# Exponent of the cumulative decays behind the key norms' logarithm, and the last products of the second rotated query part done token tile by token tile

## The chip, the cores and the metric

The kernel runs on one core of one Trainium2 chip. The metric is the device time of one execution in microseconds (us); the time before is the median of three runs. Five engines work side by side and meet through semaphores: TensorE (PE; its weight loads are PEld), VectorE (DVE), ScalarE (ACT), GpSimd (POOL) and SyncE (SP). Each engine executes its own instructions in the order in which they stand.

## The reference, cut to what matters

Two layers of an encoder on 256 tokens and 1024 channels, all in float32. A layer normalises x, multiplies it by one large matrix `w_in` and splits the result into the inputs of two branches and their gates:

```python
h = rmsnorm(x, norm_w[l])
proj = h @ w_in[l]
(q_a, k_a, v_a, ab_a, z_a, q_b, k_b, v_b, z_b, gate_a, gate_b) = jnp.split(proj, SPLIT_IDX, axis=-1)
y_a = gated_delta_branch(q_a, k_a, v_a, ab_a, z_a, ...)       # conv of width 5 + silu, l2norm, delta rule
y_b = diff_attention_branch(q_b, k_b, v_b, z_b, cos, sin, ...) # partial rotation, two softmaxes
merged = sigmoid(gate_a) * (y_a @ w_pa[l]) + sigmoid(gate_b) * (y_b @ w_pb[l])
x = x + merged @ w_out[l]
```

In the first branch, g is the running sum of the log decays inside a chunk. Its exponent scales queries and keys (`q_c * jnp.exp(g_c)`, `kb * jnp.exp(g)`), the exponents of its differences weigh the products of keys with keys and of queries with keys, and q and k are divided by their norms. In the second branch the first 16 of each 64 columns of q_b and k_b are rotated by the token's position.

## The kernel before, in words

**Products.** A float32 product is made from three products of rounded parts: high by high, high by low, low by high. `weights()` (L273) fetches 256 rows of 512 columns of the matrix as one piece `raw` through SP's queue (L304); a copy makes the high part `hi` (L308, on ScalarE, or on VectorE for the pieces listed in `turned`), and VectorE subtracts it for the low part `lo` (L310). Four such pieces, kp 0 to 3, make one projection of 512 columns; each holds two of the eight row tiles kt. There are two buffers for `hi`, two for `lo`, three for `raw`.

`proj_tm` (L315) makes a projection with tokens on the partitions. It has one accumulator in PSUM for each of the two token tiles m = 0, 1 and runs, for each kt, three products for m = 0 and three for m = 1 (L324 to L326). `proj_fm` (L374) makes a projection with features on the partitions for the convolution; its products are L385, L387 and L389. The accumulators come from a PSUM pool of four banks (`ps_p`, L81), which the big projections take in turn, two at a time. A projection can start only when the last reader of the bank that it gets is done.

**Convolution** (`conv`). Each 256-column block of an accumulator `pf_q`, `pf_k` or `pf_v` is read by one ScalarE instruction (L675, `cvq` for the queries) and by four of VectorE (L679, the other four taps, each on top of the one before; their widths are 254, 255, 255 and 254, in an order that the scheduler picks). Then come the tanh on ScalarE (L685, `thq`) and one VectorE instruction (L690, into `kq`).

**Rotated parts** (`qk_part(s_, i)`, L594; s_ = 0 queries, 1 keys; i the half of the columns). A projection `pp_qk` by `proj_tm`; ScalarE copies each accumulator to `stg` (L597), VectorE rotates it (L602 to L605), TensorE transposes it into `qkt` (L608), ScalarE copies the result to `qkT` (L610).

**Decays.** `gates()` (L754) makes the running sums of the log decays with a minus sign, `ngc`, and at its end their exponents: `E_` on ScalarE (L777; the trace calls the tile E) and `nE` = -E_ on VectorE (L778). Both are tiles of 128 x 32. `log_decays()` (L735) takes the keys' sums of squares (`ssk`), forms `kss` in a buffer that the trace calls `ge`, takes its logarithm on ScalarE (L742), and combines it with the gates and `ngc` into `lnc` (L744, L746). `decays()` (L809) takes 32 exponents of 128 x 128 tiles of `B` with `lnc` as bias (L818), held back by `cut` until the first transposes of `qk_part(0, 0)` are out; `weigh_k()` (L821) adds two of them (`dsum`) and multiplies the products of keys with keys into `A`. `E_` and `nE` are read only by the chunks of the delta rule, far later.

ScalarE has to load a table when it changes between the logarithm and the group of exponent and tanh; the compiled program holds these loads as instructions of their own, under the line of the function that needs them.

**Order.** The tile framework schedules: it takes the program below, priorities (`tc.high_priority`) and its own costs, and writes one fixed order for each engine; `behind(x)` adds a dependency on the instruction x. PSUM banks are given out in that order too. For each layer the program reads: convolution of the keys, `gates()`, a value projection, `lambdas()`, `spread()`, `log_decays()`, convolution of the queries (first half, `pf_q`), `qk_part(0, 0)`, the decays with `weigh_k`, the second half of the query convolution, `qk_part(0, 1)`, the convolution of the values (`pf_v`), `qk_part(1, 0)` and so on; after these come the z projections (`pp_zb`, `pp_za`) with the attention's scores (`sc`, L1060), their maxima (`mx`, L1068) and exponents (`es`).

Of the kernel before, what the change touches and what calls it, by code (L numbers as in the profile page):

```python
# [11 lines left out]
AF = mybir.ActivationFunctionType  # L12
ALU = mybir.AluOpType
# [4 lines left out]
P = 128  # L18
DM = 1024
KT = DM // P  # L20
# [8 lines left out]
HP = None  # L29
# [20 lines left out]
def hybrid_encoder(  # L50
# [19 lines left out]
    V, S, G, T = nc.vector, nc.scalar, nc.gpsimd, nc.tensor  # L70
# [15 lines left out]
    def bank(name):  # L86
        return ps_m.tile([P, 512], F32, tag="m", name=name)
# [10 lines left out]
    def mid(ap, n):  # L98
        return ap.unsqueeze(1).to_broadcast([ap.shape[0], n] + list(ap.shape[1:]))
# [4 lines left out]
    mark = {}  # L104
# [165 lines left out]
    def behind(ins):  # L270
        return nullcontext() if ins is None else tc.issue_after(ins)
# [41 lines left out]
                yield 2 * kp + k, hi[:, k, :n], lo[:, k, :n]  # L313

    def proj_tm(act, w, c0, n, evac, nm, places=(None,) * 4, spare=(), later=None, turned=(), between=None,  # L315
                banks=None, held=None, first=(), raws={}):

        accs = (banks or banks2)(f"pp_{nm}")
        for kt, hi, lo in weights(w, c0, n, nm, places, later=later, spare=spare, turned=turned, held=held,
                                  first=first, raws=raws):  # L320
            for m in range(NM):
                ts_ = slice(m * P, (m + 1) * P)
                o = accs[m][:, :n]
                T.matmul(o, act[kt // 4][:, 0, kt % 4, ts_], hi, start=kt == 0, stop=False)  # L324
                T.matmul(o, act[kt // 4][:, 0, kt % 4, ts_], lo, start=False, stop=False)  # L325
                mark["proj"] = T.matmul(o, act[kt // 4][:, 1, kt % 4, ts_], hi, start=False,  # L326
                                        stop=kt == KT - 1).ins
                mark["done", nm, kt] = mark["proj"]
        if between:
            between()  # L330
        for m in range(NM):
            evac(m, accs[m][:, :n])
# [174 lines left out]
    for l in range(DEPTH):  # L507
# [86 lines left out]
        def qk_part(s_, i):  # L594
                def evac_qk(m, ps):
                    st = work.tile([P, 512], F32, tag="w2a", name=f"stg{l}{s_}{i}{m}", bufs=2)
                    S.copy(st, ps)  # L597
                    g_ = st.rearrange("p (g e) -> p g e", e=DH)
                    x12 = g_[:, :, 0 : 2 * RD].rearrange("p g (x r) -> p g x r", x=2)
                    both = lambda t_: mid(mid(t_[:, m, :], 2), 8)  # L600
                    r4 = small.tile([P, 2, 8, 2, RD], F32, tag="r4", name=f"r4{l}{s_}{i}{m}", bufs=1)
                    V.tensor_tensor(r4[:, 0], x12, both(cos), ALU.mult)  # L602
                    V.tensor_tensor(r4[:, 1], x12, both(sin), ALU.mult)
                    V.tensor_tensor(x12[:, :, 0], r4[:, 0, :, 0], r4[:, 1, :, 1], ALU.subtract)
                    V.tensor_tensor(x12[:, :, 1], r4[:, 0, :, 1], r4[:, 1, :, 0], ALU.add)  # L605
                    pt = bank(f"qkt{l}{m}{s_}{i}")
                    for b in range(4):
                        T.transpose(pt[:, b * P : (b + 1) * P], st[:, b * P : (b + 1) * P], ident)  # L608

                    mark["qkT", m] = S.mul(qkT[i][:, s_, :, m * P : (m + 1) * P],  # L610
                                           pt.rearrange("p (b t) -> p b t", b=4), (DH ** -0.5, 1.0)[s_]).ins
                proj_tm(hT, wl, (C_QB, C_KB)[s_] + 512 * i, 512, evac_qk, f"qk{l}{s_}{i}",
                        turned=(0, 1) if (s_, i) == (0, 1) else ())

# [13 lines left out]
        for kt in range(KT):  # L628
            for part in range(2):
                T.matmul(abp[0:64, :SEQ], wabr[:, kt, :], hT[kt // 4][:, part, kt % 4, :],  # L630
                         start=kt == 0 and part == 0, stop=kt == KT - 1 and part == 1)
# [3 lines left out]
        for m in range(NM):  # L635
            T.matmul(abq[:, m * 32 : (m + 1) * 32], abT[:, m * P : (m + 1) * P], id2,
                     start=True, stop=True)
# [93 lines left out]
        nE = small.tile([P, 4, NH], F32, tag="nE", name=f"nE{l}")  # L731
        ngc = small.tile([P, 4, NH], F32, tag="ngc", name=f"ngc{l}")
        E_ = small.tile([P, 4, NH], F32, tag="E_", name=f"E_{l}")

        def log_decays():  # L735
            kss = e_[:, :, 32:40]
            V.tensor_scalar(kss, ssk, 4.0 * EPS, None, ALU.add)
            kh = small.tile([P, NM, NH], F32, tag="kh", name=f"kh{l}")
            V.tensor_scalar(kh, kss, 1.0 / 16.0, None, ALU.mult)
            G.tensor_tensor(nrm.rearrange("p m h -> p (m h)"), kh.rearrange("p m h -> p (m h)"),  # L740
                            phalf, ALU.pow)
            S.activation(kss, kss, AF.Ln)  # L742
            for d in range(2):
                V.scalar_tensor_tensor(lnc[:, d], ev[:, :, d * 8 : d * 8 + 8], -1.0, kss,  # L744
                                       ALU.mult, ALU.subtract)
            V.tensor_tensor(lnc.rearrange("p d c h -> p (d c) h"), lnc.rearrange("p d c h -> p (d c) h"),  # L746
                            ngc, ALU.add)
# [6 lines left out]
        def gates():  # L754
            with behind(mark[f"k{l}1", 0][0]):
                S.activation(ev, ev, AF.Ln)
            V.scalar_tensor_tensor(ev, a_, 0.0, ev, ALU.max, ALU.add)
            glog = small.tile([P, NM, 16], F32, tag="glog", name=f"glog{l}")
            V.tensor_tensor(glog, ev[:, :, 16:32], mid(nega, NM), ALU.mult)

            gr_ps = bank(f"grps{l}")
            for d in range(2):
                for c in range(NM):
                    dc = 2 * d + c
                    T.matmul(gr_ps[0:8, dc * P : (dc + 1) * P], glog[:, c, d * 8 : d * 8 + 8],
                             tri[:, d, :], start=True, stop=True)
            grow = work.tile([8, 4, P], F32, tag="w2c", name=f"grow{l}", bufs=3)
            with behind(mark[f"k{l}1", 3][1]):
                V.tensor_copy(grow.rearrange("h c i -> h (c i)"), gr_ps[0:8, :])
            gv = gdr.rearrange("c h d i -> h d c i")  # L770
            for d in range(2):
                G.dma_start(out=gv[:, d], in_=grow[:, 2 * d : 2 * d + 2])
            gc_ps = bank(f"gcps{l}")
            for dc in range(4):
                T.transpose(gc_ps[:, dc * 8 : dc * 8 + 8], grow[:, dc, :], ident[:8, :8])
            V.tensor_scalar(ngc, gc_ps[:, :32].rearrange("p (c h) -> p c h", c=4), -1.0, None, ALU.mult)
            S.activation(E_, ngc, AF.Exp, scale=-1.0)  # L777
            V.tensor_scalar(nE, E_, -1.0, None, ALU.mult)  # L778


        A = big.tile([P, 2, NM, 4, P], F32, tag="A", name=f"A{l}")
# [327 lines left out]
        def z_part(z, c_base, nm, i):  # L1109
            def evac_z(m, ps):  # L1110
                silu2(z[i][:, m, :], ps)
            proj_tm(hT, wl, c_base + 512 * i, 512, evac_z, f"{nm}{l}{i}",
                    banks=None if i or nm == "za" else banks2_c)
# [6 lines left out]
        with tc.high_priority(offset=HP):  # L1120
            gates()
        for _ in proj_by_tile(hT, wl, C_VB + 512, evac_v(1), f"vb{l}1", places2, spare=range(4),
# [4 lines left out]
                              held={} if l else dict.fromkeys(range(2), mark[f"k{l}0", 1][0])):  # L1127
            pass
        lambdas()
        spread()  # L1130
        log_decays()
        conv("q", C_QA, 1, 0)
        qk_part(0, 0)
        cut = mark["qkT", 0]
        decays(0, 0)
# [8 lines left out]
        conv("q", C_QA, 1, 1)  # L1144
        take_blocks()
        qk_part(0, 1)
        conv("v", C_VA, None, 0)
        qk_part(1, 0)
        substitute(f"qk{l}10")
        conv("v", C_VA, None, 1)  # L1150
# [141 lines left out]
        def evac_o(i):  # L1292
            def evac(m, ps, cs=slice(0, 512)):
# [7 lines left out]
                held={2: mark["load", f"pb{l}1", 1], 3: mark["load", f"pb{l}1", 3]})  # L1301
# [81 lines left out]
```

## Time and profile before

| what | value |
|---|---|
| median of three runs (751.34, 753.07, 753.03) | 753.03 us |
| the profiled execution | 751.43 us |
| its span, first to last instruction | 749.7 us |
| granted TensorE clock, mean | 0.997 |
| busy: PE, DVE, ACT, POOL | 739.6, 586.4, 480.9, 139.0 us |

The span is 1.7 us shorter than the execution's own time. Times in rows are microseconds from the span's start; a row shows start, duration, engine, line, operation, output and inputs, and in brackets for how long the engine stood idle before it and what released it. Instructions of one engine overlap a little in the rows, so that the distance from start to start is what an instruction takes from its engine's time, and it is shorter than the duration. PE is busy almost throughout, so what counts is where PE waits, and for whom.

### The profile page before, as it was taken

To read this page: it belongs to the slowest core of one execution; us is meant where nothing else is said; L and a number is where in the kernel's file an instruction comes from. 1 tells how busy PE (TensorE), PEld (TensorE's weight loads), DVE (VectorE), ACT (ScalarE), POOL (GpSimd) and SP (SyncE) were. 2 spreads that over 40 slices of the span, in tenths; PEclk is the share of its full clock that TensorE was granted. 3 is DMA by queue.
4 is the path that set the end of the run, shared out by engine and by line. 5 is a ranking of instruction groups with operands and counts; after the bars stand their busy time and mean duration, and the time that the engine had idled before them with its cause. 6 is when DMAs were issued, how large, how long until landed. Compare 5 with 4: busy or idle time off the path is not lost.

```text
span 749.7 us, 13916 instructions
## 1 busy us (share of the span) xinstructions
PE 739.6 (99%) x5176; PEld 641.2 (86%) x5176; DVE 586.4 (78%) x1109; ACT 480.9 (64%) x1022; POOL 139.0 (19%) x221
## 2 busy tenths in 40 slices
PE   8999999999999999999999999999999999999996
PEld 6999899987888889888889889889778888998885
DVE  8696898999985965578667769999999669537782
ACT  6657775667876576645456578555787757566552
POOL 5004111112022440100000150202110425301000
PEclk9999999999999999999999999999999999999998
DMA  8755566776666462567674466767666747336641
GB/s 260 238 169 169 167 171 199 212 209 198 208 182 177 151 181 84 170 199 245 202 232 134 130 189 174 216 178 233 199 171 194 197 129 234 94 114 200 218 143 57
DMA packets 73734, 135.46 MB, mean 181 GB/s; under 512 B 12944, under 2 KB 13921, under 8 KB 73666
## 3 DMA queue, kind: packets, MB, share of 16 engines
q1 hardware_dynamic: 64750, 113.65, 50.3%
q0 software_dynamic: 7936, 19.35, 8.8%
q10 hardware_dynamic: 980, 1.58, 0.6%
q8 instruction: 41, 0.67, 0.4%
q14 instruction: 27, 0.22, 0.1%
HBM read 125.53 MB, written 9.01 MB: 179 GB/s over the span
## 4 chain that ended last, share of the span: by engine, by line
PE 95%; DVE 1%; issue 1%; ACT 1%; DMA 1%; SPq 0%; POOLq 0%; POOL 0%; DVEq 0%; ACTq 0%
PE pp_vb L369 4%; PE pp_qk L325 4%; PE pp_qk L326 3%; PE pp_qk L324 3%; PE sc L1060 2%; PE pp_o L369 2%; PE pf_k L385 2%; PE pp_za L325 2%; PE pf_v L385 2%; PE pf_v L389 2%; PE pp_gb L324 2%; PE pp_gb L325 2%; PE pp_zb L324 2%; PE pf_q L387 2%; PE pf_k L387 2%; PE pf_v L387 2%
## 5 line engine op out<-in xcount | busy, mean ns | idle before, releaser
L325 PE MATMUL pp_qk<-lo_qk,hT 128*128 128x512 f32 x128 | 50.5, 395 | 1.1 <-DVE lo_qk L310 1.1
L326 PE MATMUL pp_qk<-hi_qk,hT 128*128 128x512 f32 x128 | 49.9, 390 | 0.0
L310 DVE TENSOR_TENSOR lo_qk<-raw_qk,hi_qk 128x1024 fp32r<-128x1024 f32 x32 | 39.0, 1220 | 11.8 <-ACT hi_qk L308 11.6
L324 PE MATMUL pp_qk<-hi_qk,hT 128*128 128x512 f32 x128 | 45.4, 395 | 0.0
L308 ACT CAST hi_qk<-raw_qk 128x1024 fp32r<-128x1024 f32 x28 | 29.4, 1049 | 22.9 <-PE pp_qk L326 7.1
L1070 ACT ACTIVATE es<-sc,mx 128x256 f32<-128x256 f32 x64 | 29.6, 474 | 19.6 <-DVE mx L1068 19.6
L310 DVE TENSOR_TENSOR lo_pb<-raw_pb,hi_pb 128x1024 fp32r<-128x1024 f32 x16 | 19.6, 1224 | 21.2 <-ACT hi_pb L308 20.9
L387 PE MATMUL pf_q<-hT,hi_q 128*128 128x256 f32 x128 | 36.1, 286 | 0.0
L385 PE MATMUL pf_k<-hT,hi_k 128*128 128x256 f32 x128 | 36.0, 287 | 0.0
L385 PE MATMUL pf_v<-hT,hi_v 128*128 128x256 f32 x128 | 35.8, 285 | 0.0
L387 PE MATMUL pf_v<-hT,hi_v 128*128 128x256 f32 x128 | 35.8, 284 | 0.0
L385 PE MATMUL pf_q<-hT,hi_q 128*128 128x256 f32 x128 | 35.8, 284 | 0.0
L387 PE MATMUL pf_k<-hT,hi_k 128*128 128x256 f32 x128 | 35.7, 283 | 0.0
L389 PE MATMUL pf_q<-hT,lo_q 128*128 128x256 f32 x128 | 35.1, 287 | 0.0
L389 PE MATMUL pf_v<-hT,lo_v 128*128 128x256 f32 x128 | 34.5, 287 | 0.0
L389 PE MATMUL pf_k<-hT,lo_k 128*128 128x256 f32 x128 | 34.3, 283 | 0.0
L308 ACT CAST hi_pa<-raw_pa 128x1024 fp32r<-128x1024 f32 x16 | 16.9, 1055 | 22.2 <-PE pp_pa L326 16.0
L679 DVE SCALAR_TENSOR_TENSOR cvq<-pf_q,cw,cvq 128x254 f32<-128x254 f32 (+1 forms) x64 | 29.9, 477 | 0.9 <-ACT cvq L675 0.2
L325 PEld LDWEIGHTS pp_qk<-lo_qk,hT 128*128 128x128 f32 x128 | 24.0, 188 | 7.4 <-DVE lo_qk L310 2.4
L679 DVE SCALAR_TENSOR_TENSOR cvv<-pf_v,cw,cvv 128x254 f32<-128x254 f32 (+1 forms) x64 | 29.7, 474 | 0.1
L679 DVE SCALAR_TENSOR_TENSOR cvk<-pf_k,cw,cvk 128x254 f32<-128x254 f32 (+1 forms) x64 | 29.0, 477 | 1.0 <-ACT cvk L675 0.2
L310 DVE TENSOR_TENSOR lo_pa<-raw_pa,hi_pa 128x1024 fp32r<-128x1024 f32 x16 | 19.6, 1224 | 11.2 <-ACT hi_pa L308 11.2
(414 smaller groups left out, 2536.9 us busy)
## 6 DMA issues: line engine op xcount, KB each, us to landing
raw_qk<-in_w_in_dram SPq DMA_DIRECT2D x32, 512.0 KB, 3.8
raw_k<-in_w_in_dram SPq DMA_DIRECT2D x16, 512.0 KB, 4.5
raw_q<-in_w_in_dram SPq DMA_DIRECT2D x16, 512.0 KB, 3.7
raw_v<-in_w_in_dram SPq DMA_DIRECT2D x16, 512.0 KB, 3.8
raw_zb<-in_w_in_dram SPq DMA_DIRECT2D x16, 512.0 KB, 3.7
raw_za<-in_w_in_dram SPq DMA_DIRECT2D x16, 512.0 KB, 3.7
raw_ga<-in_w_in_dram SPq DMA_DIRECT2D x16, 512.0 KB, 4.7
raw_pb<-in_w_pb_dram SPq DMA_DIRECT2D x16, 512.0 KB, 3.9
```

The source lines that it names most:

```text
L308: high = (V.tensor_copy if kp in turned else S.copy)(hi[:, :, :n], raw[:, :, :n]).ins
L310: mark[nm, kp] = high, V.tensor_tensor(lo[:, :, :n], raw[:, :, :n], hi[:, :, :n].bitcast(F32), ALU.subtract).ins
L324: T.matmul(o, act[kt // 4][:, 0, kt % 4, ts_], hi, start=kt == 0, stop=False)
L325: T.matmul(o, act[kt // 4][:, 0, kt % 4, ts_], lo, start=False, stop=False)
L326: mark["proj"] = T.matmul(o, act[kt // 4][:, 1, kt % 4, ts_], hi, start=False, stop=kt == KT - 1).ins
L369: mark["proj"] = T.matmul(o, act[kt // 4][:, pa, kt % 4, ts_], ws[kt][1 + pw], start=kt == 0 and n_ == 0, stop=kt == KT - 1 and n_ == 2).ins
L385: T.matmul(o, hi[:, cs], act[kt // 4][:, 0, kt % 4, :], start=first, stop=False, skip_group_check=True)
L387: T.matmul(o, hi[:, cs], act[kt // 4][:, 1, kt % 4, :], start=False, stop=False, skip_group_check=True)
L389: T.matmul(o, lo[:, cs], act[kt // 4][:, 0, kt % 4, :], start=False, stop=done, skip_group_check=True)
L679: V.scalar_tensor_tensor(ca[:, o0:o1], acc[:, b, o0 + sft : o1 + sft], cw[:, j, cb : cb + 1], ca[:, o0:o1], ALU.mult, ALU.add)
L1060: mm = T.matmul(sp[n][:, qt * SEQ : (qt + 1) * SEQ], qkT[h // 4][rows, 0, h % 4, qt * P : (qt + 1) * P], qkT[h // 4][rows, 1, h % 4, :], s ...
L1070: S.activation(es[:, n, qt, :], spv[:, qt, :], AF.Exp, bias=mx[:, n, qt : qt + 1], accum_out=s_all[:, h, n, qt : qt + 1])
```

## The change

Two edits. First, `E_` and `nE` leave the end of `gates()`. They now stand in `log_decays()`, right behind the logarithm of `kss`; `E_` with a dependency on that logarithm and with high priority, `nE` with neither. Second, `proj_tm` gets an argument `ends`, which only `qk_part(0, 1)` sets: the products of the last two row tiles (kt 6 and 7) are written as six for token tile 0 and then six for token tile 1, instead of three and three alternating.

```diff
     def proj_tm(..., banks=None, held=None, first=(), raws={}, ends=False):
+        ending = []
         accs = (banks or banks2)(f"pp_{nm}")
         for kt, hi, lo in weights(...):
+            last_ = [(kt, hi, lo)]
+            if ends and kt >= KT - 2:
+                ending.append((kt, hi, lo))
+                if kt < KT - 1:
+                    continue
+                last_ = ending
             for m in range(NM):
-                ts_ = slice(m * P, (m + 1) * P)
-                o = accs[m][:, :n]
-                T.matmul(...)   # three products
+                for kt, hi, lo in last_:
+                    ts_ = slice(m * P, (m + 1) * P)
+                    o = accs[m][:, :n]
+                    T.matmul(...)   # three products
...
                 proj_tm(hT, wl, (C_QB, C_KB)[s_] + 512 * i, 512, evac_qk, f"qk{l}{s_}{i}",
-                        turned=(0, 1) if (s_, i) == (0, 1) else ())
+                        turned=(0, 1) if (s_, i) == (0, 1) else (), ends=(s_, i) == (0, 1))
...
-            S.activation(kss, kss, AF.Ln)
+            with behind(S.activation(kss, kss, AF.Ln).ins), tc.high_priority(offset=HP):
+                S.activation(E_, ngc, AF.Exp, scale=-1.0)
+            V.tensor_scalar(nE, E_, -1.0, None, ALU.mult)
...
             V.tensor_scalar(ngc, gc_ps[:, :32]..., -1.0, None, ALU.mult)
-            S.activation(E_, ngc, AF.Exp, scale=-1.0)
-            V.tensor_scalar(nE, E_, -1.0, None, ALU.mult)
```

Lines behind the first edit move down by 8, so L685 becomes L693 and so on. Each engine has as many instructions as before; POOL's order is unchanged, and on SP only two loads of `raw_za` change places. On the other three engines the scheduler moves rows in many places. The following are the ones that the prediction speaks of, from layer 0.

**Place A, ScalarE, about 77 us in the trace of before: logarithm, table load, tanh of the first query block.** `ge` is the buffer of `kss`, and the number behind a name is that of a buffer. Before:

```order
L742 ACT_TABLE_LOAD
L742 ACTIVATE ge_347<-ge_347 128x2x8 [waits DVE_49]
L685 ACT_TABLE_LOAD [waits DVE_49]
L685 ACTIVATE thq_996<-cvq_990 128x256 [waits Activation_49]
L675 ACTIVATE cvq_999<-pf_q_868,cw_300 128x256
L308 CAST hi_qk_1062<-raw_qk_1064 128x1024 [waits DMAHW7_49,PE_49]
```

Now:

```order
L750 ACT_TABLE_LOAD
L750 ACTIVATE ge_347<-ge_347 128x2x8 [waits DVE_49]
L751 ACT_TABLE_LOAD
L751 ACTIVATE E_369<-ngc_368 128x32
L693 ACTIVATE thq_996<-cvq_990 128x256 [waits DVE_49,Activation_49]
L683 ACTIVATE cvq_999<-pf_q_868,cw_300 128x256
L308 CAST hi_qk_1062<-raw_qk_1064 128x1024 [waits DMAHW7_49,PE_49]
```

The second table load no longer waits for VectorE; the wait is on the tanh alone, and `E_` stands between.

**Place A, VectorE, beside it.** Before:

```order
L679 SCALAR_TENSOR_TENSOR cvq_990<-pf_q_868,cw_300,cvq_990 128x255 [waits DVE_49]
L744 SCALAR_TENSOR_TENSOR lnc_366<-ge_347 128x16 [waits Activation_49]
L744 SCALAR_TENSOR_TENSOR lnc_366<-ge_347 128x16
L679 SCALAR_TENSOR_TENSOR cvq_990<-pf_q_868,cw_300,cvq_990 128x254 [waits DVE_49]
L746 TENSOR_TENSOR lnc_366<-lnc_366,ngc_368 128x32 [waits DVE_49]
```

Now:

```order
L687 SCALAR_TENSOR_TENSOR cvq_990<-pf_q_868,cw_300,cvq_990 128x255 [waits DVE_49]
L754 SCALAR_TENSOR_TENSOR lnc_366<-ge_347 128x16 [waits Activation_49]
L754 SCALAR_TENSOR_TENSOR lnc_366<-ge_347 128x16
L752 TENSOR_SCALAR nE_367<-E_369 128x32 [waits Activation_49]
L687 SCALAR_TENSOR_TENSOR cvq_990<-pf_q_868,cw_300,cvq_990 128x254 [waits DVE_49]
L756 TENSOR_TENSOR lnc_366<-lnc_366,ngc_368 128x32 [waits DVE_49]
```

`nE`, which waits for `E_`, now stands ahead of the last tap of `cvq_990`, on which the tanh depends.

**Place C, VectorE, about 105 to 110 us: the low parts of the last two pieces of `qk_part(0, 1)` and the first block of the second query half (`cvq_1323`).** Before:

```order
L310 TENSOR_TENSOR lo_qk_1397<-raw_qk_1398,hi_qk_1396 128x1024 [waits DMAHW7_49,Activation_49]
L679 SCALAR_TENSOR_TENSOR cvq_1323<-pf_q_1201,cw_300,cvq_1323 128x255 [waits DVE_49] x2
L679 SCALAR_TENSOR_TENSOR cvq_1323<-pf_q_1201,cw_300,cvq_1323 128x254 [waits DVE_49]
L310 TENSOR_TENSOR lo_qk_1415<-raw_qk_1416,hi_qk_1414 128x1024 [waits DMAHW0_49,Activation_49]
L690 SCALAR_TENSOR_TENSOR kq_359<-thq_1329,cvq_1323 128x2x128 [waits Activation_49]
```

Now:

```order
L310 TENSOR_TENSOR lo_qk_1397<-raw_qk_1398,hi_qk_1396 128x1024 [waits DMAHW7_49,Activation_49]
L687 SCALAR_TENSOR_TENSOR cvq_1323<-pf_q_1201,cw_300,cvq_1323 128x255 [waits DVE_49]
L310 TENSOR_TENSOR lo_qk_1415<-raw_qk_1416,hi_qk_1414 128x1024 [waits DMAHW0_49,Activation_49]
L687 SCALAR_TENSOR_TENSOR cvq_1323<-pf_q_1201,cw_300,cvq_1323 128x254 [waits DVE_49]
L698 SCALAR_TENSOR_TENSOR kq_359<-thq_1329,cvq_1323 128x2x128 [waits Activation_49]
```

The last low part (`lo_qk_1415`) now stands ahead of the block's last tap. On PE, where all twelve products of kt 6 and 7 belong to that piece, token tile 0 (`pp_qk_1358`) now ends two products earlier than before, because one product of token tile 1 stays near the front. And the first products of the value convolution for the next piece (two, into the first accumulator) now stand ahead of those into the second accumulator.

**Place D, VectorE, about 174 to 178 us: two pieces of the second zb projection (`lo_zb_2192` and what stands ahead of it).** Before:

```order
L399 SCALAR_TENSOR_TENSOR zb_0_385<-zb_0_385,pp_zb_2028 128x512 [waits Activation_49]
L679 SCALAR_TENSOR_TENSOR cvv_1896<-pf_v_1741,cw_300,cvv_1896 128x254 [waits DVE_49]
L869 TENSOR_TENSOR fstmp_378<-la_375,X_377 128x255 [waits DVE_49]
L1076 SCALAR_TENSOR_TENSOR es_2106<-es_2106,cc_2120 128x256 [waits DVE_49]
L1076 SCALAR_TENSOR_TENSOR es_2106<-es_2106,cc_2120 128x256
L310 TENSOR_TENSOR lo_zb_2192<-raw_zb_2193,hi_zb_2191 128x1024 [waits DMAHW6_49,Activation_49]
```

Now:

```order
L698 SCALAR_TENSOR_TENSOR thv_1893<-thv_1893,cvv_1896 128x256 [waits Activation_49]
L878 TENSOR_TENSOR X_377<-X_377,fstmp_378 128x15x17 [waits DVE_49]
L1084 SCALAR_TENSOR_TENSOR es_2106<-es_2106,cc_2120 128x256 [waits DVE_49]
L407 SCALAR_TENSOR_TENSOR zb_0_385<-zb_0_385,pp_zb_2028 128x512 [waits Activation_49]
L1084 SCALAR_TENSOR_TENSOR es_2106<-es_2106,cc_2120 128x256
L135 STREAM_TRANSPOSE tb_v_1904<-thv_1893 128x512 [waits DMASW5_49,DMASW6_49,DMASW1_49,DMASW7_49,DMASW0_49,DVE_49]
L1076 TENSOR_REDUCE mx_2126<-sc_2128 128x2 [waits PE_49]
L310 TENSOR_TENSOR lo_zb_2192<-raw_zb_2193,hi_zb_2191 128x1024 [waits DMAHW6_49,Activation_49]
```

Counted from the program's start, four instructions that stood behind `lo_zb_2192` now stand ahead of it (`thv`, one `X`, the transpose `tb_v` of L135, and one `mx`), and none has moved the other way.

More of the change, by code (lines that the diff above doesn't have):

```diff
@@ L315, in proj_tm @@
     def proj_tm(act, w, c0, n, evac, nm, places=(None,) * 4, spare=(), later=None, turned=(), between=None,
-                banks=None, held=None, first=(), raws={}):
+                banks=None, held=None, first=(), raws={}, ends=False):
+        ending = []
         accs = (banks or banks2)(f"pp_{nm}")
@@ L320, in proj_tm @@
                                   first=first, raws=raws):
-            for m in range(NM):
-                ts_ = slice(m * P, (m + 1) * P)
-                o = accs[m][:, :n]
[L324 to L328, printed above, removed]
+            last_ = [(kt, hi, lo)]
[4 more added lines that the diff above has]
+                last_ = ending
+            for m in range(NM):
+                for kt, hi, lo in last_:
+                    ts_ = slice(m * P, (m + 1) * P)
+                    o = accs[m][:, :n]
+                    T.matmul(o, act[kt // 4][:, 0, kt % 4, ts_], hi, start=kt == 0, stop=False)
+                    T.matmul(o, act[kt // 4][:, 0, kt % 4, ts_], lo, start=False, stop=False)
+                    mark["proj"] = T.matmul(o, act[kt // 4][:, 1, kt % 4, ts_], hi, start=False,
+                                            stop=kt == KT - 1).ins
+                    mark["done", nm, kt] = mark["proj"]
         if between:
```

## The prediction

> **What bounds the kernel now.** I read first the page's busy times and its chain of work that ended last:
>
> ```profile
> PE 739.6 (99%) x5176; PEld 641.2 (86%) x5176; DVE 586.4 (78%) x1109; ACT 480.9 (64%) x1022; POOL 139.0 (19%) x221
> PE 95%; DVE 1%; issue 1%; ACT 1%; DMA 1%; SPq 0%; POOLq 0%; POOL 0%; DVEq 0%; ACTq 0%
> ```
>
> TensorE is the bound, and the change leaves its work alone. An edit elsewhere counts only where PE waits. So the next view is that of PE's waits; of its rows only this one lies near the change:
>
> ```profile
> PE pp_qk L325 <- DVE lo_qk L310: 1.1, 2, 0.5
> ```
>
> Two waits of 0.5 us, one per layer, for a low part of a weight piece. The timeline of the three engines around 76 to 83 us shows where it comes from (layer 1 repeats it). ScalarE, VectorE and PE in turn:
>
> ```profile
> 76.11 1.28 ACT L742 ACT_TABLE_LOAD   x1
> 77.41 0.22 ACT L742 ACTIVATE ge<-ge 128x16 f32<-128x16 f32 x1
> 78.38 1.28 ACT L685 ACT_TABLE_LOAD   x1 [0.76 <-DVE cvq L679]
> 79.68 0.42 ACT L685 ACTIVATE thq<-cvq 128x256 f32<-128x256 f32 x1
> 80.00 0.46 ACT L675 ACTIVATE cvq<-pf_q,cw 128x256 f32<-128x256 f32 x1
> 80.36 1.04 ACT L308 CAST hi_qk<-raw_qk 128x1024 fp32r<-128x1024 f32 x1
> ...
> 77.83 0.47 DVE L679 SCALAR_TENSOR_TENSOR cvq<-pf_q,cw,cvq 128x254 f32<-128x254 f32 x1
> 80.13 0.42 DVE L690 SCALAR_TENSOR_TENSOR kq<-thq,cvq 128x256 f32<-128x256 f32 x1 [1.72 <-ACT thq L685]
> 81.43 1.22 DVE L310 TENSOR_TENSOR lo_qk<-raw_qk,hi_qk 128x1024 fp32r<-128x1024 f32 x1
> ...
> 81.45 0.73 PE L324 MATMUL pp_qk<-hi_qk,hT 128*128 128x512 f32 x2
> 82.71 0.50 PE L325 MATMUL pp_qk<-lo_qk,hT 128*128 128x512 f32 x1 [0.52 <-DVE lo_qk L310]
> ```
>
> Read it backwards. The product at 82.71 waits for `lo_qk`, which ends at 82.65 and began as the cast `hi_qk` ended (81.40). The cast stands behind the tanh at 79.68, the tanh behind the second table load, and that load waits 0.76 us for the last tap `cvq` (77.83 + 0.47 = 78.30). Whatever moves this tanh moves PE by as much.
>
> **The change part by part.** *Place A, the exponent.* This is what `E_` and `nE` cost where they stand now, ScalarE first, then VectorE, each with its successor:
>
> ```profile
> 50.67 0.22 ACT L777 ACTIVATE E<-ngc 128x32 f32<-128x32 f32 x1
> 50.80 0.42 ACT L685 ACTIVATE thk<-cvk 128x256 f32<-128x256 f32 x1
> ...
> 51.94 0.17 DVE L778 TENSOR_SCALAR nE<-E 128x32 f32<-128x32 f32 x1
> 52.02 0.41 DVE L690 SCALAR_TENSOR_TENSOR kq<-thk,cvk 128x256 f32<-128x256 f32 x1
> ```
>
> From start to start they take 0.13 and 0.08 us, there under PE's products, so their removal there gains nothing. In the new place the second table load needs only the logarithm, which ends at 77.63; the load takes 1.30 from its start to the next (78.38 to 79.68). So `E_` runs from 78.94 to 79.16. Were the last tap done by then, the tanh would follow at 78.94 + 0.13 = 79.07, 0.61 earlier than 79.68. But VectorE now has `nE` ahead of that tap, and `nE` waits for `E_`. Two `lnc` stand there too and are done by then. `nE` starts at 79.16 + 0.03 (the hand-over from tanh to `kq`: 79.68 + 0.42 = 80.10 to 80.13), the tap 0.08 later at 79.27, ends at 79.74, and the tanh starts 0.03 to 0.08 after (0.08 is what the load needed after 78.30): 79.77 to 79.82, which is 0.09 to 0.14 *later*. The load is hidden and the tap that it hid behind is exposed in its place. Behind `nE` on VectorE are queued the tap, the last `lnc` and the products of `kq`; the wait of PE grows by the same amount. I take **+0.12 us per layer**. The bounds: -0.8 if the wait goes (82.71 less 81.45 and two products of 0.23, the distance of PE's starts 112.50 to 112.73 below), and +0.14.
>
> One more price is in this place. The rows show no time lost at a table load: the cast ahead of the first ends at 76.10 (75.05 + 1.05) and the load starts at 76.11, the logarithm 0.02 after the load's end.
>
> ```profile
> 75.05 1.05 ACT L308 CAST hi_qk<-raw_qk 128x1024 fp32r<-128x1024 f32 x1
> ```
>
> The Trainium skill ("ScalarE: Activation LUTs", section "What ACT_TABLE_LOAD costs") says otherwise: a switch is the load of about 1.28 us and a drain of about 1.38 us. By it, with the drain between logarithm and load, the sum here would be some 1.4 us per layer worse, an estimate from that page. The trace agrees with its 1.28 and shows none of the drain behind a cast or ahead of a logarithm; behind a logarithm it cannot tell, as the load there waited anyway. That is a rival below.
>
> *Place B, about 91 to 108 us.* The transposes of `qk_part(0, 0)`'s first token tile now stand 18 `pf_q` products later on PE, which at up to 0.13 each (twelve of `pf_v` from 113.11 to 114.65 below) is up to 2.3 us, and the 32 exponents of the decays wait for them. ScalarE's rows, then the low part they delay and its reader:
>
> ```profile
> 92.33 2.44 ACT L818 ACTIVATE B<-B,lnc 128x128 f32<-128x128 f32 x8
> 104.13 1.05 ACT L308 CAST hi_qk<-raw_qk 128x1024 fp32r<-128x1024 f32 x1 [1.16 <-issue]
> 105.58 1.22 DVE L310 TENSOR_TENSOR lo_qk<-raw_qk,hi_qk 128x1024 fp32r<-128x1024 f32 x1
> 107.97 0.39 PE L325 MATMUL pp_qk<-lo_qk,hT 128*128 128x512 f32 x1
> ```
>
> The cover: ScalarE stood idle 1.16 ahead of the cast, and `lo_qk` ended 1.17 (107.97 less 106.80) before PE read it. A delay of 2.3 less the 0.3 of one tanh moved ahead (108.67 to 108.98 below) is 2.0, under 2.3. I cost it at nothing; with half the cover gone it is up to 0.9 per layer.
>
> *Place C, the ends of `qk_part(0, 1)`.* ScalarE, VectorE, PE:
>
> ```profile
> 108.67 0.41 ACT L685 ACTIVATE thq<-cvq 128x256 f32<-128x256 f32 x1
> 108.98 0.46 ACT L675 ACTIVATE cvq<-pf_q,cw 128x256 f32<-128x256 f32 x1
> 110.48 1.05 ACT L308 CAST hi_v<-raw_v 128x1024 fp32r<-128x1024 f32 x1 [1.04 <-issue]
> 111.44 0.46 ACT L675 ACTIVATE cvq<-pf_q,cw 128x256 f32<-128x256 f32 x1
> 112.47 0.59 ACT L597 COPY stg<-pp_qk 128x512 f32<-128x512 f32 x1 [0.57 <-PE pp_qk L326]
> ...
> 108.80 1.23 DVE L310 TENSOR_TENSOR lo_qk<-raw_qk,hi_qk 128x1024 fp32r<-128x1024 f32 x1 [0.57 <-ACT hi_qk L308]
> 109.94 0.42 DVE L690 SCALAR_TENSOR_TENSOR kq<-thq,cvq 128x256 f32<-128x256 f32 x1
> 112.84 0.86 DVE L679 SCALAR_TENSOR_TENSOR cvq<-pf_q,cw,cvq 128x254 f32<-128x254 f32 x2
> ...
> 112.50 0.39 PE L325 MATMUL pp_qk<-lo_qk,hT 128*128 128x512 f32 x1
> 112.73 0.39 PE L326 MATMUL pp_qk<-hi_qk,hT 128*128 128x512 f32 x1
> 113.11 0.39 PE L385 MATMUL pf_v<-hT,hi_v 128*128 128x256 f32 x1
> 114.65 0.28 PE L385 MATMUL pf_v<-hT,hi_v 128*128 128x256 f32 x1
> ```
>
> `pf_v` takes over the bank of token tile 0, so its first product waits for the copy `stg` that ends at 113.06: 112.73 to 113.11 is 0.15 more than the usual 0.23. That 0.15 is all that `ends` can win. Tile 0 ends two products (0.45) earlier. But ScalarE is now late: `lo_qk` stands ahead of the last tap, so the tap starts at 109.94, ends at 110.41 and the tanh starts at 110.44 instead of 108.67. With the rows' distances (tanh to `cvq` 0.31, `cvq` to the next 0.36, cast to `cvq` 0.96, `cvq` to the next 0.36) `stg` starts at 112.43 instead of 112.47. Of the 0.45, 0.04 is left.
>
> The second accumulator (114.65) takes the bank of the first query block pair, whose last reader is the second `cvq` of the row at 112.84, done at 113.70: 0.95 to spare. That chain now starts 1.77 later, with the low part of `pf_v` and two rotation products on VectorE between its taps; I get its end at about 114.98. The order puts two products (0.25) ahead of the second accumulator, so PE needs it at 114.90: 0.1 late. Together **+0.1 us per layer**, between -0.15 and +0.6 (the chain's delay of 1.77 less the 0.95 and the 0.25).
>
> *Place D, the z projections.* VectorE's pieces and the PE product that reads `lo_zb`:
>
> ```profile
> 155.86 1.23 DVE L310 TENSOR_TENSOR lo_qk<-raw_qk,hi_qk 128x1024 fp32r<-128x1024 f32 x1 [0.81 <-ACT hi_qk L308]
> 176.00 1.22 DVE L310 TENSOR_TENSOR lo_zb<-raw_zb,hi_zb 128x1024 fp32r<-128x1024 f32 x1
> 177.94 0.48 PE L325 MATMUL pp_zb<-lo_zb,hT 128*128 128x512 f32 x1
> L135 DVE STREAM_TRANSPOSE tb_v<-thv 128x512 f32<-128x512 f32 x8 | 5.6, 698 | 0.0
> L1068 DVE TENSOR_REDUCE mx<-sc 128x2 f32<-128x512 f32 x32 | 21.0, 682 | 0.0
> ```
>
> Four instructions more stand ahead of `lo_zb`: 0.70, 0.68, and for `thv` and `X` the 0.42 of `kq`, which is as wide, less 0.08 of overlap each (as `nE` and `kq` overlap at 52.02): 1.9 us. VectorE's last idle time before, 0.81, can take some of it, so `lo_zb` ends 1.1 to 1.9 later than 177.22, at 178.3 to 179.1. PE by then is 0.2 to 0.3 late itself and needs it at 178.2: a new wait of 0.1 to 0.9, or none if VectorE has more room earlier. I take **+0.3 us per layer**, nearer the low end since the idle time is filled first. The two loads that SP exchanges belong to `raw_za`, later pieces than these; nothing for them.
>
> **The sum.** 0.12 + 0.1 + 0.3 = 0.52 per layer, about +1.0 us for two. The profiled execution of 751.43 becomes 752.5; the median is 1.6 above that execution, so 753.03 becomes **754.1 us**. A measurement of this kernel tells some 0.3%, 2.3 us, from no change: the forecast lies within that.
>
> **The rivals.**
>
> 1. *The waits go.* VectorE or ScalarE run ahead of the rows, the tap is in time, and the waits of places A and C vanish: up to 0.8 + 0.15 per layer, 1.9 us, giving 751.1; half of it 752.1. For it: the table load itself is truly hidden. Against it: the order of VectorE, in which `nE` cannot start before 79.19. Even then the gain is under 0.3%. Chance 0.16.
> 2. *Slower: the late decays.* Place B loses its cover: the exponents come 2.3 us later, ScalarE reaches the casts `hi_qk` of `qk_part(0, 1)` late, and PE waits for the low part at 107.97. Price: 2.3 less the 1.17 of the low part is 1.1 per layer, with the terms above 3.2 us: 756.2. It decides once the cast ends more than 2.3 us after the 105.18 of before. For it: VectorE's `A` products must also come first and wait for PE. Against: 1.16 idle and the 1.17. Chance 0.10.
> 3. *Slower: the load is not free behind a logarithm.* The load at 78.38 shows only that it could start by then, so it may start up to 0.74 later than 77.64, and everything in place A with it: 0.74 per layer, 1.5 in all, with the sum 755.6. This is the mechanism of the skill's page named above. Chance 0.05.
> 4. *The change does less than it says.* The order shows that `ends` moves tile 0 by two products, not three, and the logarithm and the exponent do stand together; this is in the forecast already.
>
> **How the numbers follow.** The forecast has 0.69; with its terms at their upper ends (0.14, 0.6 and 0.9, or 3.3 in all) it passes 2.3 us in a small part, 0.06. Slower by over 0.3% is that with 0.08 of rival 2 and 0.03 of rival 3: 0.17. Faster by over 0.3% needs both waits gone and something more, 0.04 from rival 1. The rest, 0.79, is within 0.3%. The range goes from rival 1 (751.1) to the upper ends and rival 2 (756.3): 751.1 to 756.3.
>
> **What would show it.** Right: the tanh behind `E_` starts 2.2 us (79.8 less 77.63) after the logarithm's end in both layers, `nE` with an idle time ahead of it on VectorE that ends on `E`; PE's wait for `lo_qk` in place A is 0.6 to 0.7, not 0.5; `stg` starts no earlier than before against PE; a new wait of PE for `lo_zb`. Wrong: the wait `lo_qk` gone from PE's list; a wait of over 0.5 us at the products of `qk_part(0, 1)` or at `pf_v`'s second accumulator; no wait at `lo_zb`; or a table load that starts later than 0.1 us after the logarithm.

## The result, and the profile after

| | before | after |
|---|---|---|
| median of 11 runs each | 751.48 us (751.18 to 753.07) | 754.25 us (753.52 to 756.77) |
| ratio, with its 95% interval | 1 | 1.0041 (1.0033 to 1.0049) |
| the profiled execution, its span | 751.43, 749.7 us | 754.24, 752.5 us |
| granted TensorE clock | 0.997 | 0.998 |

The changed kernel is slower by 0.4%, 2.8 us, in the medians and in the two profiled executions alike. That the forecast of 754.1 lies near 754.25 is luck: its difference, +1.0 us, was put on a median of three (753.03), which eight more runs brought down to 751.48. The measured difference is nearly three times the forecast one, and the profiled execution, forecast at 752.5, came at 754.24.

The page of after, its busy times and the chain of work that ended last:

```profile
PE 741.6 (99%) x5176; PEld 641.8 (85%) x5176; DVE 587.4 (78%) x1109; ACT 482.2 (64%) x1022; POOL 139.8 (19%) x221
PE 74%; DVE 5%; ACT 1%; issue 1%; DMA 1%; POOL 0%; POOLq 0%; DVEq 0%; ACTq 0%
```

TensorE has the instructions that it had and is still the bound. In the chain PE went from 95% to 74% and VectorE from 1% to 5%; but the shares of after add up to only 82%, those of before to 99%, so this chain was not followed over the whole span. In a second profile of the same kernel (the sixth experiment) they add up to 99%, with 84% for PE, 4% each for VectorE, DMA and issue, and 2% for ScalarE. PE's waits name the tiles (engine, line, waited for: us in total, times, longest):

```profile
PE pp_qk L333 <- DVE lo_qk L310: 1.5, 3, 0.5
...
PE pp_zb L333 <- DVE lo_zb L310: 0.5, 1, 0.5
```

Before, `lo_qk` had 1.1 in two waits and `lo_zb` none. This list counts only the idle time that PE shows; how far PE falls behind is read from the starts of the same product in both traces. Place by place:

**Place A**, the timeline of after; ScalarE, VectorE, then PE:

```profile
77.22 0.21 ACT L750 ACTIVATE ge<-ge 128x16 f32<-128x16 f32 x1
77.45 1.28 ACT L751 ACT_TABLE_LOAD   x1
78.74 0.23 ACT L751 ACTIVATE E<-ngc 128x32 f32<-128x32 f32 x1
79.67 0.42 ACT L693 ACTIVATE thq<-cvq 128x256 f32<-128x256 f32 x1 [0.70 <-DVE lnc L756]
...
79.00 0.18 DVE L752 TENSOR_SCALAR nE<-E 128x32 f32<-128x32 f32 x1 [1.28 <-ACT E L751]
...
80.91 0.39 PE L334 MATMUL pp_qk<-hi_qk,hT 128*128 128x512 f32 x1
81.44 0.73 PE L332 MATMUL pp_qk<-hi_qk,hT 128*128 128x512 f32 x2
82.70 0.50 PE L333 MATMUL pp_qk<-lo_qk,hT 128*128 128x512 f32 x1 [0.53 <-DVE lo_qk L310]
```

The load starts 0.02 us after the logarithm (77.43), so it is hidden; but `nE` holds VectorE idle for 1.28 us ahead of the tap (which starts at 79.10), and the tanh comes 2.24 us after the logarithm's end, where before it came 2.05 after (79.68 less 77.63). This execution's first products started earlier, and it was 0.19 ahead of before when it reached the place (80.91 here, 81.10 there for the product ahead of the row at 81.45) and 0.01 ahead behind it (82.70 to 82.71): PE lost 0.18 here.

**Places B and C**, the same view; ScalarE, VectorE and PE:

```profile
110.44 0.42 ACT L693 ACTIVATE thq<-cvq 128x256 f32<-128x256 f32 x1 [1.75 <-DVE cvq L687]
112.42 0.58 ACT L605 COPY stg<-pp_qk 128x512 f32<-128x512 f32 x1
...
112.19 1.23 DVE L310 TENSOR_TENSOR lo_v<-raw_v,hi_v 128x1024 fp32r<-128x1024 f32 x1
...
107.91 0.40 PE L333 MATMUL pp_qk<-lo_qk,hT 128*128 128x512 f32 x1
112.68 0.39 PE L334 MATMUL pp_qk<-hi_qk,hT 128*128 128x512 f32 x1
113.06 0.39 PE L393 MATMUL pf_v<-hT,hi_v 128*128 128x256 f32 x1
113.47 0.39 PE L397 MATMUL pf_v<-hT,lo_v 128*128 128x256 f32 x1
114.88 0.28 PE L395 MATMUL pf_v<-hT,hi_v 128*128 128x256 f32 x1
115.05 0.39 PE L393 MATMUL pf_v<-hT,hi_v 128*128 128x256 f32 x1
115.28 0.28 PE L395 MATMUL pf_v<-hT,hi_v 128*128 128x256 f32 x1
```

The first low product of before:

```profile
113.45 0.28 PE L389 MATMUL pf_v<-hT,lo_v 128*128 128x256 f32 x1
```

The product at 107.91 did not wait: the cover of place B held. The tap, the tanh and `stg` are late as the prediction has it, `stg` ends at 113.00, and `pf_v` still starts 0.38 after the product ahead of it, as before (112.73 to 113.11). The second accumulator starts 0.17 after the product ahead of it, and the product behind it 0.23 later (115.05 to 115.28), against 0.12 for the others of their kind: 0.15 or so. And there is a loss that the prediction did not ask about. The late ScalarE also makes the cast `hi_v` late, and so `lo_v`: it ends at 113.42, where before it ended at 112.91 (111.70 + 1.21). The product that reads it starts at 113.47, the one behind it at 113.70; from the first product of `pf_v` that is 0.64, before it was 0.46 (113.11 to 113.57). PE lost 0.18 there. Together with the second accumulator, PE went from 0.05 ahead of before to 0.25 behind it. Layer 1 has the same two steps, and so have the other two executions with this order of VectorE that were compared here (the first and the sixth experiment).

**A wait that nobody had looked for**, layer 0, 121 to 130 us of after:

```profile
121.18 1.05 ACT L308 CAST hi_v<-raw_v 128x1024 fp32r<-128x1024 f32 x1 [1.99 <-DMA raw_v<-in_w_in_dram]
...
122.26 1.23 DVE L310 TENSOR_TENSOR lo_v<-raw_v,hi_v 128x1024 fp32r<-128x1024 f32 x1 [1.81 <-ACT hi_v L308]
128.62 1.22 DVE L310 TENSOR_TENSOR lo_qk<-raw_qk,hi_qk 128x1024 fp32r<-128x1024 f32 x1
...
128.78 0.61 PE L332 MATMUL pp_qk<-hi_qk,hT 128*128 128x512 f32 x2
129.89 0.50 PE L333 MATMUL pp_qk<-lo_qk,hT 128*128 128x512 f32 x1 [0.49 <-DVE lo_qk L310]
```

The same two products of before:

```profile
128.34 0.61 PE L324 MATMUL pp_qk<-hi_qk,hT 128*128 128x512 f32 x2
128.79 0.50 PE L325 MATMUL pp_qk<-lo_qk,hT 128*128 128x512 f32 x1
```

PE is 0.44 late ahead of this place and 1.10 behind it. A 512 KB load of `raw_v` took 7.7 us from issue to landing where before it took 6.0, so ScalarE's cast, VectorE's low part and everything queued behind that came late.

**Place D**, layer 0 and then layer 1 of after:

```profile
163.59 1.28 ACT L734 ACTIVATE vtm<-tb_v,nrm 128x128 f32<-128x128 f32 x4 [0.30 <-DMA tb_v<-bnc_v]
178.26 1.21 DVE L310 TENSOR_TENSOR lo_zb<-raw_zb,hi_zb 128x1024 fp32r<-128x1024 f32 x1
178.79 0.60 PE L1095 MATMUL at<-ident,es 128*128 128x128 f32 x4
179.52 0.50 PE L333 MATMUL pp_zb<-lo_zb,hT 128*128 128x512 f32 x1
...
531.56 1.28 ACT L734 ACTIVATE vtm<-tb_v,nrm 128x128 f32<-128x128 f32 x4 [0.98 <-DMA tb_v<-bnc_v]
546.19 0.60 PE L1095 MATMUL at<-ident,es 128*128 128x128 f32 x4
547.32 0.50 PE L333 MATMUL pp_zb<-lo_zb,hT 128*128 128x512 f32 x1 [0.53 <-DVE lo_zb L310]
```

The rows of before that stand for the same work:

```profile
161.65 1.28 ACT L726 ACTIVATE vtm<-tb_v,nrm 128x128 f32<-128x128 f32 x4
177.58 0.60 PE L1087 MATMUL at<-ident,es 128*128 128x128 f32 x4
...
544.15 0.60 PE L1087 MATMUL at<-ident,es 128*128 128x128 f32 x4
544.50 0.48 PE L325 MATMUL pp_zb<-lo_zb,hT 128*128 128x512 f32 x1
```

From the last transposes `at` to the `lo_zb` product it is 0.36 us before (177.58 to 177.94) and 0.73 after; 0.35 before and 1.13 after in layer 1. PE loses 0.37 and 0.78. And ScalarE's `vtm`, the copy of a block of values that goes through DRAM (`bnc_v`) and back, waits for that DMA, which it did not before.

Put together, PE against before, from pairs of starts in the two traces:

| place | layer 0 | layer 1 |
|---|---|---|
| on reaching A | -0.19 | +1.61 (449.23 to 447.62) |
| behind A | -0.01 | +1.79 (451.02 to 449.23) |
| ahead of C, at the first `pf_v` | -0.05 | +1.73 (481.44 to 479.71) |
| behind C | +0.25 (119.78 to 119.53) | +2.04 (487.12 to 485.08) |
| ahead of the wait at 129 | +0.44 | |
| behind it | +1.10 | |
| ahead of D | +1.21 | +2.04 |
| behind D | +1.58 | +2.82 |

The last number is the whole loss. Of the rise from -0.19 to +2.82, 3.0 us, A has 0.36, C 0.6, D 1.15 and the wait at 129 0.66. The late `raw_v` took another 0.19 at the product that reads its low part, at 123.54 us (`lo_v` ends at 123.49), so that PE went from 0.25 late to 0.44. Under 0.1 is left.

### The profile page after: what moved, and what is told of

Read it like the earlier page. It is cut to its first block, busy times and chain, and to the rows that moved or that the text cites. A ratio compares the mean times of both kernels' runs of the same rounds, so it can differ in the third digit from the quotient of the medians.

```text
span 752.5 us, 13919 instructions
## 1 busy us (share of the span) xinstructions
PE 741.6 (99%) x5176; PEld 641.8 (85%) x5176; DVE 587.4 (78%) x1109; ACT 482.2 (64%) x1022; POOL 139.8 (19%) x221
## 3 DMA queue, kind: packets, MB, share of 16 engines
q10 hardware_dynamic: 980, 1.58, 0.6%
## 4 chain that ended last, share of the span: by engine, by line
PE 74%; DVE 5%; ACT 1%; issue 1%; DMA 1%; POOL 0%; POOLq 0%; DVEq 0%; ACTq 0%
PE pp_vb L377 3%; PE pp_o L377 2%; PE pp_qk L333 2%; PE pp_za L333 2%; PE pp_qk L334 2%; PE pp_gb L333 2%; PE pp_gb L332 2%; PE pp_ga L332 2%; PE pp_ga L333 2%; PE pp_za L332 2%; PE pp_za L334 2%; PE pp_gb L334 2%; PE pp_pb L333 2%; PE pp_ga L334 2%; PE pp_pb L334 2%; PE pp_qk L332 2%
```

## The experiments

The theory after this reading: the exponent edit costs A's 0.2 per layer by itself, and the rest comes with the other order that the scheduler writes on TensorE, VectorE and ScalarE because of it. Rivals: `ends` is what disturbs the order; or the table load behind a logarithm costs more than its row shows. All times are medians; "before" is the kernel before, run on the same chip in the same job. How far an order differs from that of before is counted in rows of VectorE that stand elsewhere, each counted twice, where it left and where it came.

**The exponent edit alone.** The argument `ends` is not set.

```diff
-                        turned=(0, 1) if (s_, i) == (0, 1) else (), ends=(s_, i) == (0, 1))
+                        turned=(0, 1) if (s_, i) == (0, 1) else ())
```

> The exponent and nE behind the logarithm, without the token-tile order of the last products. Theory (the exponent edit carries the whole loss: nE holds the last tap back in place A, and the scheduler's new order costs the rest in places C to D): as the changed kernel, +2.5 to +2.9 us against before. Rival (the token-tile order of the last products carries half or more of the loss): +0.5 to +1.4 us.

Measured: 754.69 us against 751.42, ratio 1.0044 (1.0032 to 1.0057). PE's waits in its trace:

```profile
PE pp_zb L333 <- DVE lo_zb L310: 1.2, 3, 0.5
...
PE pp_qk L333 <- DVE lo_qk L310: 1.1, 2, 0.5
```

The exponent edit carries the whole loss. VectorE's order differs from before's in 268 places here, as many as in the changed kernel: the disturbance is not that of `ends`. The wait at 129 us is gone, those at place D are more, and the sum is the same.

**`ends` alone**, on the kernel before (the diff of the second edit, without the first).

> The token-tile order alone, the exponent at the end of gates() as before. Theory: only two products change places on PE, token tile 0 ends 0.45 us earlier, and pf_v's first product loses its 0.15 us per layer: 0 to -0.3 us against before. Rival (this order costs on its own): +1 us or more.

Measured: 750.67 us against 751.42, ratio 0.9999 (0.9990 to 1.0007): no difference that the times show; they spread from 750.39 to 752.56, too widely for half a microsecond. VectorE's order is that of before throughout. In its trace `stg` starts at 111.70, and `pf_v` no longer waits for it:

```profile
112.40 0.39 PE L334 MATMUL pp_qk<-hi_qk,hT 128*128 128x512 f32 x1
112.63 0.28 PE L393 MATMUL pf_v<-hT,hi_v 128*128 128x256 f32 x1
```

0.23 instead of 0.38 us: `ends` does win what the prediction called all that it could, if nothing delays ScalarE. PE's starts against before show a step of -0.27 there, in both layers.

**The exponent early, its negative late** (exponent edit alone, `nE` written behind `qk_part(0, 0)` with a dependency on the last instruction of the convolution).

```diff
-            V.tensor_scalar(nE, E_, -1.0, None, ALU.mult)
...
+        with behind(mark["conv"]):
+            V.tensor_scalar(nE, E_, -1.0, None, ALU.mult)
```

> As the exponent edit alone, but nE is put behind the last instruction of the first half of the query convolution, so that the last tap no longer stands behind it. Theory (the hold on the tap is the cause): the tanh starts 0.5 to 0.6 us earlier than in before, PE's wait for lo_qk in place A goes, the order of places B to D stays that of before: -1.0 to -1.6 us against before. Rival (the loss is in the moved table load or in the exponent itself, whatever nE does): +0.3 to +2.8 us.

Measured: 750.23 us against 751.42, ratio 0.9986 (0.9978 to 0.9995): faster, by 1.2 us. ScalarE and PE at place A:

```profile
78.93 0.23 ACT L751 ACTIVATE E<-ngc 128x32 f32<-128x32 f32 x1
79.06 0.40 ACT L693 ACTIVATE thq<-cvq 128x256 f32<-128x256 f32 x1
...
82.08 0.50 PE L333 MATMUL pp_qk<-lo_qk,hT 128*128 128x512 f32 x1
```

The tanh starts at 79.06, where the prediction has it "were the last tap done by then" (79.07). It is 0.62 ahead of before, and PE's product 0.63; the wait for `lo_qk` is gone from PE's list. In this kernel only `nE` stands elsewhere on VectorE (4 places, two a layer). So one instruction's place, `nE` ahead of the tap, both eats the gain of A and sets off the other 264.

**Both edits, with the negative late.** The same edit on the changed kernel, `ends` kept.

> The whole change with nE put behind the first half of the query convolution. Theory: both gains add, -1.0 to -1.9 us against before, and pf_v's wait for the copy stg is gone. Rival (the two edits work against each other, as ScalarE comes late to stg): no better than the same kernel without the token-tile order, within 0.1 us of it.

Measured: 749.67 us against 751.42, ratio 0.9975 (0.9965 to 0.9984). It beats both kernels: 1.75 us under the one before. `pf_v` follows without a wait, the view as above:

```profile
112.39 0.39 PE L334 MATMUL pp_qk<-hi_qk,hT 128*128 128x512 f32 x1
112.61 0.28 PE L393 MATMUL pf_v<-hT,hi_v 128*128 128x256 f32 x1
```

PE's starts against before show steps of -0.62 at A and -0.27 at C in both layers: twice 0.89 is 1.78. Of the 0.27, the 0.15 of `pf_v`'s first product is the part that the rows above name; the rest is in the product behind it, which follows after 0.12 (112.61 to 112.73) where before it took 0.23 (113.11 to 113.34).

**The whole change, with the order held.** One low part of the second query half on VectorE waits for the rotation of token tile 0 of `qk_part(0, 0)`, which it overtakes in the changed kernel. `nE` stays ahead of the tap.

```diff
+                if nm in ("q01", "q11") and kp == 1:
+                    dve = mark["rot"]
...
-                    V.tensor_tensor(x12[:, :, 1], r4[:, 0, :, 1], r4[:, 1, :, 0], ALU.add)
+                    rot = V.tensor_tensor(x12[:, :, 1], r4[:, 0, :, 1], r4[:, 1, :, 0], ALU.add).ins
+                    if (s_, i, m) == (0, 0, 0):
+                        mark["rot"] = rot
```

> The whole change, nE still ahead of the last tap, and one dependency more: the low part of the second piece of the second query half waits for the rotation of token tile 0 of qk_part(0, 0), as it stood in before. With it the order of places B to D is again that of before, in both layers. Theory (the hold on the tap costs only place A, and the rest of the loss is the order that the scheduler chose because of it): place A +0.36, the token-tile order -0.3, so -0.4 to +0.5 us against before, and the waits at lo_zb are gone. Rival (the hold itself, by delaying everything behind it, makes the waits of C and D): +2.0 to +2.8 us as in the changed kernel.

Measured: 751.43 us against 751.47, ratio 0.9999 (0.9989 to 1.0008). With this one dependency the order differs from before's in 12 places instead of 268, and 2.8 us are gone, while place A is as in the changed kernel (`nE` idle for 1.28, the tanh 0.92 behind the start of `E_`; 0.93 in the changed kernel). PE has its two waits for `lo_qk` back, 1.1 us, and none for `lo_zb`. PE is 0.18 later behind A, as in the changed kernel, and gains the 0.27 of `ends` at C. Against the kernel above, from which its order on VectorE differs in `nE`, one tap and one low part per layer, it is 1.76 slower: 0.88 per layer, near the 0.62 + 0.18 = 0.80 of the rows. So A by itself costs 0.2 per layer and forgoes 0.6, and the rest of the loss against before is the work of the order.

**The changed kernel again**, to see what of its waits comes back.

> The changed kernel once more, for a second profile. Theory (the layer 0 wait for lo_qk near 129 us comes from one late landing of raw_v, which meets the loads of la and lt, and so differs from run to run): +2.2 to +2.9 us, the waits at lo_zb again 0.3 and 0.7 us, the wait near 129 us gone or of another size. Rival (it belongs to the order): the same 0.65 us there.

Measured: 754.67 us against 751.47, ratio 1.0036 (1.0022 to 1.0049). Casts and waits, ScalarE, VectorE, PE:

```profile
120.15 1.05 ACT L308 CAST hi_v<-raw_v 128x1024 fp32r<-128x1024 f32 x1 [0.81 <-DMA raw_v<-in_w_in_dram]
163.77 1.28 ACT L734 ACTIVATE vtm<-tb_v,nrm 128x128 f32<-128x128 f32 x4 [1.42 <-DMA tb_v<-bnc_v]
...
178.26 1.20 DVE L310 TENSOR_TENSOR lo_zb<-raw_zb,hi_zb 128x1024 fp32r<-128x1024 f32 x1
```

The load of `raw_v` is 1.0 us earlier this time, and there is no wait at 129 us. But ScalarE's wait for the DMA grew from 0.30 to 1.42, `lo_zb` starts at the same 178.26, and PE is as late as before when D is over: by 192 us it is 1.62 late in both executions and 1.63 in the one with the exponent edit alone (medians over 2 us of the starts of the same products). Whatever these three had lost by 156 us (1.22, 0.29 and 0.95), they lost the rest of 1.6 at D. What they share is the start of `vtm` behind its DMA, at 163.59, 163.77 and 163.76, and not the waits ahead of it.

**The copies of the values later.** `vtm` of the second block of values is placed behind the fourth piece of the zb projection instead of the second, so that ScalarE's casts `hi_zb` don't queue behind its DMA.

```diff
-                place_v(mark[f"zb{l}0", 1][0])
+                place_v(mark[f"zb{l}0", 3][0])
```

> The changed kernel, but ScalarE's four copies vtm of the second value block, which wait for that block's way through DRAM, stand behind the fourth cast of the first zb projection, so that a tanh of the value convolution, two casts and a first tap no longer queue behind them. The four VectorE instructions that the prediction counted still stand ahead of the second zb projection's second low part. Theory (the waits at lo_zb come from ScalarE standing still for the DMA ahead of the tanh): ScalarE's wait for tb_v goes or falls on work that nobody waits for, PE's waits at lo_zb fall by more than half, +0.8 to +1.8 us against before. Rival (the four instructions ahead of the low part make the waits, as the prediction had it): the waits at lo_zb stay, +2.3 to +3.3 us.

Measured: 753.55 us against 751.49, ratio 1.0024 (1.0013 to 1.0035). Its rows at place D:

```profile
167.63 1.28 ACT L734 ACTIVATE vtm<-tb_v,nrm 128x128 f32<-128x128 f32 x4
...
178.55 0.60 PE L1095 MATMUL at<-ident,es 128*128 128x128 f32 x4
179.30 0.50 PE L333 MATMUL pp_zb<-lo_zb,hT 128*128 128x512 f32 x1
```

ScalarE no longer waits for the DMA, and of 3.2 us (the run above) or 2.8 (the result) 2.1 are left, between what the theory and its rival expected. `at` to the `lo_zb` product is still 0.75. So the wait of `vtm` is a part of the loss, some 0.35 to 0.55 us per layer (half of 2.8 or 3.2 less 2.1), and another part, 0.75 less the 0.36 of before, stays with the instructions that VectorE now has ahead of `lo_zb`. A and C still cost what they cost in the changed kernel, 1.0 for both layers together. The intervals of this run and of the changed kernel overlap a little (1.0033 to 1.0049 and 1.0013 to 1.0035), so the split is rough.

## Why the prediction was right and wrong

**Place A: right.** The forecast was +0.12 per layer, measured 0.18 in both. The load is hidden, `nE` is idle in wait for `E`, and the tanh starts 2.24 after the logarithm's end (2.2 forecast). One detail differs: the wait for `lo_qk` did not grow to 0.6 or 0.7 but stayed at 0.53; what PE lost lies one product earlier, where it waits for the cast (80.91 to 81.44 is 0.53, before 81.10 to 81.45 is 0.35). The bound of -0.8 was real too: without `nE` ahead of the tap it is -0.62.

**Place B: right.** Its cover held.

**Place C: the steps right, the sum too small.** The tanh at 110.44 and `stg` at 112.42 stand where the working put them (110.44, 112.43), and the second accumulator costs some 0.15, near the 0.1 forecast. But the working followed the late ScalarE to `stg` and to that accumulator only, and not through the cast `hi_v` to `lo_v`, whose first product cost another 0.18. C took 0.3 per layer where +0.1 was forecast; its bound of 0.6 held. The exponent edit alone loses the same there, and with the order held PE loses nothing at C. That `ends` can win 0.15 and no more was too low: where nothing delays ScalarE it won 0.27 per layer.

**Place D: the step that failed, in its size.** "I take +0.3 us per layer, nearer the low end since the idle time is filled first." The mechanism, a new wait for `lo_zb` behind four more instructions of VectorE, was there, and where ScalarE does not wait it costs about what was said, 0.4. But the working took only VectorE's queue. ScalarE's queue had a DMA in it, and the new order starts that DMA later. The tile's instructions before, then in the changed kernel run again (times of first and last start):

```profile
L142 POOL DMA_DIRECT2D tb_v<-bnc_v x4: 548/548/558, 153.9 to 155.6; - x4
L135 DVE STREAM_TRANSPOSE tb_v<-thv x2: 697/700/703, 149.5 to 166.5; 128x512 f32<-128x512 f32 x2
```

```profile
L142 POOL DMA_DIRECT2D tb_v<-bnc_v x4: 551/551/561, 157.1 to 158.7; - x4
L135 DVE STREAM_TRANSPOSE tb_v<-thv x2: 703/704/705, 153.3 to 166.1; 128x512 f32<-128x512 f32 x2
```

The transpose of the second block of values went from 149.5 to 153.3 us, the reads back from DRAM by as much as 3.2, and `vtm` with the casts `hi_zb` behind it had to wait. D took 0.37 and 0.78 per layer in one execution. In the other PE went from 0.29 late to 1.60 over D in layer 0, 1.3 us: 0.5 at the `lo_zb` product of 168.33, which the working did not name, and 0.8 at the one that it did. At its own product the upper bound of 0.9 held; for the z projections as a whole it was broken.

**The wait at 129 us was not in the working at all.** It took 0.66 in one of two executions of the changed kernel, and the same late load 0.19 ahead of it. It adds nothing to the total where D fills up to the same point anyway. Why `lo_qk` had so little room there in layer 0 (0.05 us before: 127.52 + 1.22 against 128.79) was in the trace of before and could have been read.

**The rivals.** Rival 1, the waits go, did not happen; with `nE` late it does, and wins 1.75 us, near the 1.9 at which it was priced. Rival 2, the late decays: no wait at 107.91, refuted. Rival 3, a load that is not free behind a logarithm: refuted by 77.43 to 77.45, and by `E_` at 78.74, 0.01 after the load's end. The Trainium skill ("ScalarE: Activation LUTs", section "What ACT_TABLE_LOAD costs") gives a drain of some 1.38 us beside each load of 1.28; the load agrees, and behind a logarithm, as behind a cast, this trace leaves room for 0.02. Rival 4 was in the forecast: `ends` gave nothing in the changed kernel (754.25 with it, 754.69 without it, intervals overlapping).

**The chances.** Slower by over 0.3% is what came, and it had 0.17. The terms at their upper ends, 3.3 us in all, were given 0.06, though the working of place D knew only one of the two queues that lead to `lo_zb`. An order that differs in 268 places on VectorE called for more.

## What to carry to other kernels

A table load is hidden by putting an instruction of the next table, whose operands are long there, right behind the last one of the old table. But look at once where its consumers stand on the other engines: an in-order queue that meets such a consumer too early hands the load's time on to everything behind it, and here moving one 0.1 us instruction back turned a loss of 2.8 us into a gain of 1.75.

Where a scheduler writes the order, count the rows that moved for an edit; when a small edit moves hundreds, hold the order with one dependency before judging the edit. And follow both queues that lead to a late operand, with the DMA round trips in them, not only the last engine's.

## What the runs showed that was not expected

Two executions of one kernel can lose the same time at different places: PE was 1.22 and 0.29 late at 156 us and 1.62 late in both at 192. The DMA round trip through DRAM ended at nearly the same time (`vtm` starts at 163.59 and 163.77), although its last read was issued 0.9 us apart (159.6 and 158.7). So a wait's place in one profile is weaker evidence than the total behind the last common point.
